# Modulation products of a two-layer hybrid backbone: units of 256 columns behind every second block instead of units of 128 behind every block

## The chip, the cores and the metric

The kernel runs on one core of one Trainium2 chip. Times are device microseconds (us) of that core; the metric is the median time of several executions. Traces are of single executions, and "span" is the time in the trace from the first to the last instruction. The engines are called PE (TensorE), DVE (VectorE), ACT (ScalarE), POOL (GpSimd) and SP (the queue from which nearly all transfers are issued).

## The reference, cut to what matters

Two layers work on 512 latent and 256 context tokens of width 1024. Each layer normalizes its input, applies a modulation, projects it, runs three mixers side by side (mLSTM, attention, gated DeltaNet), merges them, and runs a gated MLP. The modulation comes from one small vector for the latent tokens and one for the context tokens:

```python
silu_c = jax.nn.silu(c)                    # (1, 1024)
silu_cc = jax.nn.silu(c_ctx)               # (1024,)
for l in range(2):
    m_lat = split(silu_c  @ ada_w[l] + ada_b[l], 6)   # ada_w[l]: (1024, 6144)
    m_ctx = split(silu_cc @ ada_w[l] + ada_b[l], 6)
    xn = modulate(rmsnorm(h, norm1_w[l]), m[0], m[1])
    h = h + m[2] * merge_branches(...)
    h = h + m[5] * conv_ffn(modulate(rmsnorm(h, norm2_w[l]), m[3], m[4]), ...)
```

All of it is float32. The two modulation vectors of a layer are products of a 2 x 1024 with a 1024 x 6144 matrix: 24 MB of weights per layer for two rows of output. The products of the tokens (768 rows) with the other weights are the large products.

## The kernel before, in words

**Large products.** `gemm_fm` (L227) walks over blocks of 128 output columns. For each block it loads the weights into a buffer of the ring `wraw` (L207, three buffers of 128 x 1024 float32), splits them into a high and a low part (ACT and DVE), and issues three matmuls per 128 rows of depth (`mm3`, L241; the lines L248, L249 and L250): high x high, high x low and low x high, over 512 latent columns and, where the context is needed, 256 context columns. `gemm_first` and `gemm_tail` (L283 to L285, L313 to L315) do the same at the ends of a stage.

**Modulation products.** The first 16 groups of 128 columns of layer 0 are computed at the start in four pieces of 512 columns (`ada_mm`, L438, transposed at L449). The other 80 groups stand in a list, `adaq`, and each is a *unit* (`ada_unit`, L457): one load of 512 KB (1024 rows by 128 columns, runs of 512 bytes) into a buffer of the same ring `wraw`; eight matmuls (L467), which hold 32 columns of the condition vectors as the stationary operand and stream 128 columns of weights, each on one of four strips of 32 columns of the array, so that four of them run side by side; and a copy by ACT (L470) of the 128 x 128 result from PSUM to SBUF. Each matmul of float32 is two passes in the trace, so a unit is 16 rows of PE. The unit is finished by `ada_fin` (L481), which is called at the beginning of the next unit: one transpose on PE (L489), and on DVE a sum over the four strips (L491) and, after every eighth group, the bias.

**Where the units stand.** A counter, `nada`, is set ahead of a stage, and `gemm_fm` issues one unit behind each block of large products until it is zero: 32 in the mixers of layer 0, 16 in the MLP of layer 0, 20 in the mixers of layer 1. `ada_fill(4)` (L473) issues four units in a row at three places: after each layer's merge, and at the start of layer 1's mixers. That makes the 80. The results of a unit go into the PSUM buffers `pc` (one buffer, which the large products of the mixers use for the context) and, for the transposes, `pl` or `pa`.

**What sets the order.** Apart from the start, the order of instructions on each engine is written out by a planner when the program is built: it simulates the engines with a cost of its own for each instruction and takes, at each step, the instruction of the highest priority that is ready. In the mixers the recurrences and the attention have a higher priority than the large products and the units, so their small matmuls are put between the matmuls of a unit wherever the planner has them ready; a unit is then *cut* into pieces. On the chip each engine executes its list in order.

**Names in the rows.** `ad` is the loaded weight buffer of a unit, `adp` the PSUM result of its matmuls, `adr` the copy, `adc` the transposed result, `ada` the modulation vector. `mg`, `cz`, `ao`, `aq`, `ak` are large products of the mixers, `f0...` those of layer 0's MLP, `b0...` attention, `c0...` gated DeltaNet, `m0...` mLSTM (0 is the layer).

Of the kernel before, what the change touches and what calls it, by code (L numbers as in the profile page):

```python
# [19 lines left out]
DEPTH = 2  # L20
NT = SEQ + CTX
KD = D // 128
# [71 lines left out]
class Kernel:  # L94
# [112 lines left out]

    def wraw(self, src, nk, ncols, nm, slot=None):

        t = slot(nm) if slot else self.T([128, 1024], nm, tag="wraw", bufs=3)  # L210
        v = t[:, : nk * ncols].rearrange("p (k c) -> p k c", k=nk)
        with self.high(self.prio):
            self.nc.sync.dma_start(v, src.rearrange("(k p) c -> p k c", p=128))
        return v
# [12 lines left out]
    def gemm_fm(self, src, c0, ncols, nk, segs, done, nm):  # L227

        for b in range(ncols // 128):
            raw = self.wraw(src[:, c0 + 128 * b: c0 + 128 * b + 128], nk, 128, f"{nm}r{b}")
            hv, lv = self.wsplit(raw, nk, 128, f"{nm}s{b}")
            done(b, self.mm3(hv, lv, nk, segs, f"{nm}p{b}"))
            if self.nada:
                self.nada -= 1
                self.ada_unit()
                if self.nada == 0:
                    self.ada_fin()

    def mm3(self, hv, lv, nk, segs, nm):  # L241
        nc = self.nc
# [214 lines left out]
    def ada_unit(self):  # L457


        nc = self.nc  # L460
        l, g = self.adaq.pop(0)
        raw = self.wraw(self.I["ada_w"][l][:, 128 * g:128 * g + 128], KD, 128, f"ad{l}_{g}")
        self.ada_fin()
        ps = self.adps[0](f"adp{l}_{g}")
        for k in range(KD):
            j = k % 4
            nc.tensor.matmul(ps[32 * j:32 * j + 32, 0:128], self.s32[:, 2 * k:2 * k + 32], raw[:, k, :],  # L467
                             start=(k < 4), stop=(k >= 4), tile_position=(0, 32 * j))
        rw = self.T([128, 128], f"adr{l}_{g}", tag="adr")
        nc.scalar.copy(rw, ps[:, 0:128])  # L470
        self.adal = (l, g, rw)

    def ada_fill(self, n):  # L473

        if n:
# [2 lines left out]
                self.ada_unit()  # L478
            self.ada_fin()

    def ada_fin(self):  # L481

        nc = self.nc
        if self.adal is None:
            return
        l, g, rw = self.adal
        self.adal = None
        ps = self.adps[1](f"adc{l}_{g}")
        nc.tensor.transpose(ps[:, 128:256], rw, self.ident)  # L489
        a = self.ada[l][:, g:g + 1, :]  # L490
        nc.vector.tensor_reduce(out=a, in_=ps[:, 128:256].rearrange("p (o j r) -> p o r j", o=1, j=4)[:, :, 0:2, :],  # L491
                                axis=AX.X, op=ALU.add)
        if g % 8 == 7:
            a = self.ada[l][:, g - 7:g + 1, :]
            bb = self.vcol("ab", 48 * l + g - 7, 8)
            nc.vector.tensor_tensor(out=a, in0=a, in1=bb.rearrange("p (b o) -> p b o", o=1).broadcast_to([128, 8, 2]),
                                    op=ALU.add)

# [166 lines left out]
    def gates_mm(self, l, xs, gc):  # L665

        nc = self.nc
        nm = f"g{l}"
        W = self.I["w_in"][l]
        n = 288  # L670
        h, lo = [self.gw(f"{nm}w{u}", u).rearrange("p (k c) -> p k c", k=KD) for u in range(2)]
        for k0 in (0, 3, 6):
            nk = min(3, KD - k0)
            raw = self.T([128, 1024], f"{nm}raw{k0}", tag="wraw", bufs=3)[:, :nk * n].rearrange("p (k c) -> p k c", k=nk)
            rows = W[128 * k0:128 * (k0 + nk), :].rearrange("(k p) c -> p k c", p=128)
            for o, c0, m in ((0, A_G, 16), (16, C_G, 16), (32, B_Q + 512, 256)):
                nc.sync.dma_start(raw[:, :, o:o + m], rows[:, :, c0:c0 + m])
            self.split(h[:, k0:k0 + nk], lo[:, k0:k0 + nk], raw)
        self.bp = self.dr.tile([6, 128, 768], F32, name=f"bp{l}", tag=f"bp{l}")

        banks = ((self.pb, self.pb, self.pl), (self.pl, self.pc, self.pb)) if l else ((self.pl, self.pl, self.pc),) * 2
        for r in range(2):
            pss = [p(f"{nm}ps{r}_{i}")[:, 0:n] for i, p in enumerate(banks[r])]
            for i, ps in enumerate(pss):
                tt = 3 * r + i
                (a, _), xh, xl = xs[tt // 4]
                t = slice(128 * tt - a, 128 * tt - a + 128)
                for k in range(KD):
                    nc.tensor.matmul(ps, xh[:, k, t], h[:, k, :], start=(k == 0), stop=False)
                    nc.tensor.matmul(ps, xl[:, k, t], h[:, k, :], start=False, stop=False)  # L690
                    nc.tensor.matmul(ps, xh[:, k, t], lo[:, k, :], start=False, stop=(k == KD - 1))
                nc.vector.tensor_copy(gc[:, tt, :], ps[:, 0:32])
                if tt % 2 == 0:
                    s = self.gs(f"{nm}kv{tt}")
                nc.scalar.copy(s[:, 256 * (tt % 2):256 * (tt % 2) + 256], ps[:, 32:n])
                if tt % 2:
                    nc.sync.dma_start(self.bp[tt - 1:tt + 1, :, 512:768].rearrange("t p c -> p t c"),
                                      s.rearrange("p (t c) -> p t c", t=2))
# [1072 lines left out]
    def start(self):  # L1771

        nc = self.nc
        self.setup()
        self.load_x()
        self.adaq = [(l, g) for l in range(DEPTH) for g in range(48)][16:]
        xs = self.N["xs"]
        ws = []

        def weights(q):  # L1780
            raw = self.wraw(self.I["w_in"][0][512 * q:512 * q + 512, C_K:C_K + 256], 4, 256, f"c00kr{q}")
            ws.append(self.wsplit(raw, 4, 256, f"c00ks{q}", nc.gpsimd))

        self.fw = lambda k, b: [w[:, k % 4, 128 * b:128 * b + 128] for w in ws[k // 4]]
        segs = [(a, a + 256) for a in (0, 256, 512)]
        self.ada_mm(0, 2)
        self.norm_t(2)
        self.ada_red(0, 2)
        self.ada_mm(0, 0)
        weights(0)  # L1790
        self.ada_red(0, 0)
        self.mod_half(0)
        self.first_open(xs, "c00k")
        for i in (0, 1):
            self.norm_half(0, *segs[i])
            self.norm_low(0, *segs[i])
            self.first_part(xs, KD, 0, 4, *segs[i])
        self.norm_half(0, *segs[2])
        self.ada_mm(0, 3)
        self.spill_h(0, NT, nc.scalar)  # L1800
        self.norm_low(0, *segs[2])
        weights(1)
        self.ada_mm(0, 1)
        self.ada_red(0, 3)
        self.first_part(xs, KD, 0, 2, *segs[2])
        self.ada_red(0, 1)
        self.mod_half(1)
        self.first_part(xs, KD, 2, 4, *segs[2])
        for seg in segs:
            self.norm_half(1, *seg)  # L1810
            self.norm_low(1, *seg)
            self.first_part(xs, KD, 4, 8, *seg)

    def body(self):
        nc, tc = self.nc, self.tc
        with tc.tile_pool(name="t0", bufs=1, reuse_waits="tile") as self.ph:
            with tc.manual_schedule(engines={E.PE, E.DVE, E.Activation}):
                self.start()
            xs = self.N["xs"]
        for l in range(DEPTH):  # L1820
            nt = NT if l < DEPTH - 1 else SEQ
            with tc.tile_pool(name=f"m{l}", bufs=1, reuse_waits="tile") as self.ph:
                self.px = self.pc
                if l:
                    self.ada_fill(4)
                self.mixers(l, xs, nt)
            for i, k in enumerate(("ya", "yb", "yc")):
                if f"{k}{l}" in self.dbg:
                    nc.sync.dma_start(self.dbg[f"{k}{l}"][:, :, :nt], self.yd[i][:, :, :nt])
            with tc.tile_pool(name=f"t{l + 1}", bufs=1, reuse_waits="tile") as self.ph:  # L1830
                self.px = self.pb
                xs = self.merge(l, xs, nt)
                self.dump_h(f"h{l}", nt)
                if l + 1 < DEPTH:
                    self.ada_fill(4)
                    self.nada, self.adps = 16, (self.pc, self.pa)
                else:
                    self.ada_fill(4)
                self.spare = nt < NT
                xs = self.ffn(l, xs, nt)  # L1840
                self.dump_h(f"hf{l}", nt)
                if l + 1 < DEPTH:
                    self.spill_h(l + 1, NT, nc.sync)
# [80 lines left out]
```

## Time and profile before

| | |
|---|---|
| three executions | median 2715.18 us (2710.06 to 2716.42) |
| the profiled execution | 2712.51 us |
| its span | 2710.7 us |
| PE busy | 2640.8 us, 97% of the span |
| DVE, ACT, POOL busy | 58%, 37%, 10% |
| matmul rows of the units (L467) | 1280, 66.8 us busy |
| transposes of the units (L489) | 80 |
| loads of the units | 80 of 512 KB (96 with those of the start) |

Busy time of a group is the time covered by at least one of its instructions, so four matmuls side by side count once. The start times of consecutive rows of PE tell more than their durations: an instruction's row goes on after the next one has begun. "Idle before" is the time the engine stood still ahead of an instruction, and the name behind the arrow is what ended it.

### The profile page before, as it was taken

How to read it: one execution, taken by the hardware profiler on the slowest of the kernel's cores; microseconds unless marked ns; L12 is line 12 of the kernel's file. 1: busy time of each engine (PE TensorE's matmuls, PEld its weight loads, DVE VectorE, ACT ScalarE, POOL GpSimd, SP SyncE). 2: the span in 40 equal slices, each digit the busy share in tenths (PEclk: the TensorE clock that was granted, in tenths of full speed). 3: DMA queues.
4: the chain of work that ended last, by engine and by line, in shares of the span. 5: the costliest groups of instructions: out<-in, count | busy, mean ns of one | idle time of the engine just before them, and what ended most of it. 6: DMA issues, size and time to landing. Idle time of an engine off the chain costs nothing.

```text
span 2710.7 us, 46057 instructions
## 1 busy us (share of the span) xinstructions
PE 2640.8 (97%) x18041; PEld 2252.5 (83%) x18041; DVE 1576.0 (58%) x3517; ACT 1000.3 (37%) x2269; POOL 267.0 (10%) x262
## 2 busy tenths in 40 slices
PE   7999999999999999999999999999999999999999
PEld 5887988788888888888888889788877878888887
DVE  6676655756424656444444486766677646655555
ACT  4434355333322234232232254434633332433332
POOL 1000000000210410010010120000000103100000
PEclk9999999999999999999999999999999999999999
DMA  7354332556647423412212153522377675333332
GB/s 273 96 165 137 87 109 81 148 149 189 195 137 247 140 77 113 135 53 79 63 51 75 53 151 110 159 73 78 96 195 212 175 235 161 116 96 93 94 98 86
DMA packets 526187, 344.29 MB, mean 127 GB/s; under 512 B 48167, under 2 KB 491281, under 8 KB 525201
## 3 DMA queue, kind: packets, MB, share of 16 engines
q1 hardware_dynamic: 525681, 338.19, 42.6%
q8 instruction: 142, 2.33, 0.3%
q10 hardware_dynamic: 288, 3.15, 0.3%
q14 instruction: 76, 0.62, 0.1%
HBM read 285.23 MB, written 56.03 MB: 126 GB/s over the span
## 4 chain that ended last, share of the span: by engine, by line
PE 84%; DMA 7%; DVE 6%; ACT 1%; issue 1%; SPq 1%; POOL 0%; ACTq 0%; DVEq 0%; POOLq 0%
PE mg04p L248 2%; PE mg04p L250 2%; PE mg04p L249 2%; PE adp L467 2%; PE y0p L248 1%; PE y0p L249 1%; PE y0p L250 1%; PE mg14p L248 1%; PE mg14p L250 1%; PE mg14p L249 1%; PE y1p L248 1%; PE y0op L248 1%; PE y0op L250 1%; PE y0op L249 1%; PE y1p L249 1%
## 5 line engine op out<-in xcount | busy, mean ns | idle before, releaser
L1723 POOL TENSOR_TENSOR f0a<-f0a,f0g 128x768 f32<-128x768 f32 x22 | 40.6, 1848 | 486.4 <-DVE f0a L1711 486.4
L467 PE MATMUL adp<-ad,s 128*32 128x128 f32 x1280 | 66.8, 282 | 4.4 <-DVE cz0t L904 2.4
L1723 POOL TENSOR_TENSOR f1a<-f1a,f1g 128x512 f32<-128x512 f32 x22 | 28.5, 1294 | 313.3 <-DVE f1a L1711 303.5
L467 PEld LDWEIGHTS adp<-ad,s 128*32 128x32 f32 x1280 | 34.1, 109 | 28.1 <-issue 9.5
L1725 DVE TENSOR_TENSOR f0gl<-f0a,f0gh 128x768 fp32r<-128x768 f32 x22 | 21.1, 958 | 61.4 <-ACT f0gh L1724 61.3
L1724 ACT CAST f0gh<-f0a 128x768 fp32r<-128x768 f32 x22 | 18.4, 835 | 80.0 <-POOL f0a L1723 80.0
L1647 POOL TENSOR_TENSOR y0a<-y0a,y0g 128x768 f32<-128x768 f32 x16 | 33.0, 2063 | 128.0 <-DVE y0g L1644 125.7
L902 ACT ACTIVATE mg0t<-mg04p 128x512 f32<-128x512 f32 (+1 forms) x40 | 19.4, 486 | 40.6 <-PE mg04p L250 31.9
L470 ACT COPY adr<-adp 128x128 f32<-128x128 f32 x80 | 21.2, 265 | 33.4 <-PE adp L467 32.8
L1647 POOL TENSOR_TENSOR y1a<-y1a,y1g 128x512 f32<-128x512 f32 x16 | 23.9, 1494 | 75.6 <-DVE y1g L1644 75.3
L1717 ACT ACTIVATE f0g<-f0g 128x768 f32<-128x768 f32 x22 | 18.5, 846 | 32.9 <-DVE f0g L1711 32.9
L998 POOL TENSOR_TENSOR m0qz<-m0qz,m0e 64x512 f32<-64x512 f32 x12 | 15.4, 1282 | 151.9 <-DMA m0e<-g0rd 115.2
L1644 DVE SCALAR_TENSOR_TENSOR y0g<-y0g,y0p 128x512 f32<-128x512 f32 (+1 forms) x32 | 17.4, 550 | 15.4 <-PE y0p L250 14.6
L1717 ACT ACTIVATE f1g<-f1g 128x512 f32<-128x512 f32 x22 | 13.8, 632 | 32.9 <-DVE f1g L1711 32.9
L491 DVE TENSOR_REDUCE ada<-adc 128x2 f32<-128x8 f32 x80 | 12.9, 161 | 21.6 <-PE adc L489 21.3
L987 DVE SCALAR_TENSOR_TENSOR m0mb<-m0mb,g0a,cst 128x128 f32<-128x128 f32 x48 | 14.1, 346 | 18.7 <-DMA m0mb<-g0rd 18.6
L1668 DVE SCALAR_TENSOR_TENSOR hr<-y0op,y0gh,hr 128x512 f32<-128x512 f32 (+1 forms) x16 | 9.8, 615 | 21.1 <-PE y0op L250 21.1
L489 PE MATMUL adc<-cst,adr 128*128 128x128 f32 x80 | 21.9, 273 | 0.0
L1620 DVE TENSOR_TENSOR y0l<-y0ld,y0h 128x768 fp32r<-128x768 f32 x12 | 13.0, 1093 | 12.6 <-ACT y0h L1619 12.5
L1011 PE MATMUL m0n<-m0vb,m0mb 128*128 128x129 f32 x96 | 18.1, 279 | 1.2 <-issue 1.2
L1743 DVE SCALAR_TENSOR_TENSOR hr<-f0d4p,ada,hr 128x512 f32<-128x512 f32 (+1 forms) x16 | 9.9, 618 | 15.7 <-PE f0d4p L250 15.7
L1743 DVE SCALAR_TENSOR_TENSOR hr<-f0d8p,ada,hr 128x512 f32<-128x512 f32 (+1 forms) x16 | 9.9, 618 | 15.7 <-PE f0d8p L250 15.7
(3924 smaller groups left out, 9948.7 us busy)
## 6 DMA issues: line engine op xcount, KB each, us to landing
ad<-ada_w SPq DMA_DIRECT2D x96, 512.0 KB, 4.1
mg04r<-w_in SPq DMA_DIRECT2D x20, 512.0 KB, 4.2
mg14r<-w_in SPq DMA_DIRECT2D x20, 512.0 KB, 4.7
y0g<-mg SPq DMA_DIRECT2D x24, 384.0 KB, 3.7
mg<-mg0t SPq DMA_DIRECT2D x24, 256.0 KB, 2.3
y0r<-w_branch SPq DMA_DIRECT2D x12, 512.0 KB, 4.7
mg<-mg1t SPq DMA_DIRECT2D x24, 256.0 KB, 3.4
y1r<-w_branch SPq DMA_DIRECT2D x12, 512.0 KB, 4.2
```

The costliest lines, as they stand in the source:

```text
L248: nc.tensor.matmul(o, hv[:, k, :], xh[:, k, :], start=(k == 0), stop=False)
L249: nc.tensor.matmul(o, hv[:, k, :], xl[:, k, :], start=False, stop=False)
L250: nc.tensor.matmul(o, lv[:, k, :], xh[:, k, :], start=False, stop=(k == nk - 1))
L467: nc.tensor.matmul(ps[32 * j:32 * j + 32, 0:128], self.s32[:, 2 * k:2 * k + 32], raw[:, k, :], start=(k < 4), stop=(k >= 4), tile_position ...
L470: nc.scalar.copy(rw, ps[:, 0:128])
L489: nc.tensor.transpose(ps[:, 128:256], rw, self.ident)
L902: nc.scalar.activation(s, o, AF.Tanh, scale=0.5)
L1647: nc.gpsimd.tensor_tensor(out=a[:, :nt], in0=a[:, :nt], in1=gt[:, :nt], op=ALU.add)
L1717: nc.scalar.activation(a[:, :nt], a[:, :nt], AF.Silu)
L1723: nc.gpsimd.tensor_tensor(out=a[:, :nt], in0=a[:, :nt], in1=keep[b][:, :nt], op=ALU.mult)
L1725: nc.vector.tensor_tensor(out=gl[:, k, :nt], in0=a[:, :nt], in1=gh[:, k, :nt].bitcast(F32), op=ALU.subtract)
L1743: nc.vector.scalar_tensor_tensor(out=hv[:, a:b], in0=ps, scalar=self.ada[l][:, 40 + j, (a >= SEQ):(a >= SEQ) + 1], in1=hv[:, a:b], op0=ALU ...
```

## The change

A unit is made twice as wide: 256 columns of the modulation weights, loaded in two transfers of 512 rows each (512 KB each, runs of 1024 bytes). Its eight matmuls stream 256 columns instead of 128, ACT copies 128 x 256, PE makes two transposes and DVE sums both in one instruction. There are 40 such units instead of 80. A unit stands behind every second block of large products (the counter keeps its values 32, 16 and 20 and counts blocks), `ada_fill` is called with 2 instead of 4, and the ring `wraw` has four buffers instead of three.

```diff
-        t = slot(nm) if slot else self.T([128, 1024], nm, tag="wraw", bufs=3)
+        t = slot(nm) if slot else self.T([128, 1024], nm, tag="wraw", bufs=4)
...
             done(b, self.mm3(hv, lv, nk, segs, f"{nm}p{b}"))
-            if self.nada:
-                self.nada -= 1
-                self.ada_unit()
-                if self.nada == 0:
-                    self.ada_fin()
+            self.ada_next()
...
-        raw = self.wraw(self.I["ada_w"][l][:, 128 * g:128 * g + 128], KD, 128, f"ad{l}_{g}")
+        W = self.I["ada_w"][l]
+        raws = [self.wraw(W[512 * q:512 * q + 512, 256 * g:256 * g + 256], 4, 256, f"ad{l}_{g}_{q}") for q in range(2)]
         self.ada_fin()
         ps = self.adps[0](f"adp{l}_{g}")
-        for k in range(KD):
-            j = k % 4
-            nc.tensor.matmul(ps[32 * j:32 * j + 32, 0:128], self.s32[:, 2 * k:2 * k + 32], raw[:, k, :],
-                             start=(k < 4), stop=(k >= 4), tile_position=(0, 32 * j))
-        rw = self.T([128, 128], f"adr{l}_{g}", tag="adr")
-        nc.scalar.copy(rw, ps[:, 0:128])
+        for q, raw in enumerate(raws):
+            for j in range(4):
+                k = 4 * q + j
+                nc.tensor.matmul(ps[32 * j:32 * j + 32, 0:256], self.s32[:, 2 * k:2 * k + 32], raw[:, j, :],
+                                 start=(q == 0), stop=(q == 1), tile_position=(0, 32 * j))
+        rw = self.T([128, 256], f"adr{l}_{g}", tag="adr")
+        nc.scalar.copy(rw, ps[:, 0:256])
...
+    def ada_next(self):
+        if self.nada:
+            self.nada -= 1
+            if self.nada % 2:
+                self.ada_unit()
+            if self.nada == 0:
+                self.ada_fin()
...
-        nc.tensor.transpose(ps[:, 128:256], rw, self.ident)
-        a = self.ada[l][:, g:g + 1, :]
-        nc.vector.tensor_reduce(out=a, in_=ps[:, 128:256].rearrange("p (o j r) -> p o r j", o=1, j=4)[:, :, 0:2, :],
+        for b in range(2):
+            nc.tensor.transpose(ps[:, 256 + 128 * b:384 + 128 * b], rw[:, 128 * b:128 * b + 128], self.ident)
+        nc.vector.tensor_reduce(out=self.ada[l][:, 2 * g:2 * g + 2, :],
+                                in_=ps[:, 256:512].rearrange("p (o j r) -> p o r j", o=2, j=4)[:, :, 0:2, :],
                                 axis=AX.X, op=ALU.add)
-        if g % 8 == 7:
+        if g % 4 == 3:
...
-        self.adaq = [(l, g) for l in range(DEPTH) for g in range(48)][16:]
+        self.adaq = [(l, g) for l in range(DEPTH) for g in range(24)][8:]
...
-                    self.ada_fill(4)
+                    self.ada_fill(2)
```

## Rows read from the trace of the kernel before

**Rows 1.** The page: busy time, share of the span and instructions of each engine
```profile
PE 2640.8 (97%) x18041; PEld 2252.5 (83%) x18041; DVE 1576.0 (58%) x3517; ACT 1000.3 (37%) x2269; POOL 267.0 (10%) x262
```

**Rows 2.** The page: the chain that ended last, share of the span by engine
```profile
PE 84%; DMA 7%; DVE 6%; ACT 1%; issue 1%; SPq 1%; POOL 0%; ACTq 0%; DVEq 0%; POOLq 0%
```

**Rows 3.** Stages: stretch, its us, busy us per engine (instructions), clock, DMA share, GB/s
```profile
185.00:760.00 575.00, 555.65 (x4783) 472.80 (x4784) 353.30 (x976) 233.78 (x696) 36.89 (x42) 0.99 0.49 139
760.00:1010.00 250.00, 250.00 (x1490) 221.39 (x1490) 115.15 (x176) 67.40 (x111) 49.73 (x32) 1.00 0.47 151
1945.00:2165.00 220.00, 210.23 (x1746) 169.03 (x1744) 148.51 (x448) 79.89 (x224) 21.37 (x28) 0.99 0.70 194
```

**Rows 4.** The page's groups: operation, tiles, count | busy us, mean ns | idle before
```profile
L467 PE MATMUL adp<-ad,s 128*32 128x128 f32 x1280 | 66.8, 282 | 4.4 <-DVE cz0t L904 2.4
L470 ACT COPY adr<-adp 128x128 f32<-128x128 f32 x80 | 21.2, 265 | 33.4 <-PE adp L467 32.8
L491 DVE TENSOR_REDUCE ada<-adc 128x2 f32<-128x8 f32 x80 | 12.9, 161 | 21.6 <-PE adc L489 21.3
```

**Rows 5.** PE in order of time, one whole unit in the MLP: start, us, instruction
```profile
1070.53 0.28 PE L250 MATMUL f0g02p<-n01xh,f0g02s1l 128*128 128x256 f32 x1
1070.65 0.27 PE L489 MATMUL adc<-cst,adr 128*128 128x128 f32 x1
1070.85 0.65 PE L467 MATMUL adp<-ad,s 128*32 128x128 f32 x16
1071.42 0.50 PE L248 MATMUL f0a02p<-n01xh,f0a02s0h 128*128 128x512 f32 x1
1071.76 0.40 PE L249 MATMUL f0a02p<-n01xl,f0a02s0h 128*128 128x512 f32 x1
```

**Rows 6.** PE in order of time, 32 passes of 512 columns at the start
```profile
42.09 3.64 PE L438 MATMUL ad<-ad,s 128*32 128x512 f32 x32
45.66 0.66 PE L449 MATMUL adc<-cst,adr 128*128 128x128 f32 x4
46.08 0.37 PE L283 MATMUL c00kp<-n00xh,c00ks0h 128*128 128x256 f32 x1
46.28 0.28 PE L284 MATMUL c00kp<-n00xh,c00ks0l 128*128 128x256 f32 x1
```

**Rows 7.** PE in order of time, one unit of the mixers cut into three pieces
```profile
268.50 0.39 PE L250 MATMUL ak0p<-n00xh,ak0s1l 128*128 128x512 f32 x1
268.73 0.40 PE L248 MATMUL ak0p<-n00xh,ak0s1h 128*128 128x512 f32 x1
269.06 0.41 PE L467 MATMUL adp<-ad,s 128*32 128x128 f32 x4
269.40 0.71 PE L1436 MATMUL c00sp<-c00v,c00kL 128*128 128x128 f32 x4
...
270.94 0.41 PE L467 MATMUL adp<-ad,s 128*32 128x128 f32 x2
271.27 0.66 PE L1220 MATMUL b0a5pp<-cst,b0a5P 128*128 128x128 f32 x4
271.86 0.62 PE L467 MATMUL adp<-ad,s 128*32 128x128 f32 x10
272.41 0.50 PE L249 MATMUL ak0p<-n00xl,ak0s1h 128*128 128x512 f32 x1
```

**Rows 8.** PE in order of time: the first and the last of the 121 pieces
```profile
187.10 0.64 PE L467 MATMUL adp<-ad,s 128*32 128x128 f32 x16 [2.40 <-DVE cz0t L904]
2342.24 0.64 PE L467 MATMUL adp<-ad,s 128*32 128x128 f32 x16
```

**Rows 9.** Waits of PE around the units: us in total, times, longest
```profile
PE adp L467 <- DVE cz0t L904: 2.4, 1, 2.4
PE adp L467 <- ACT mg0t L902: 1.2, 1, 1.2
PE adp L467 <- DMA ad<-ada_w: 0.8, 1, 0.8
```

**Rows 10.** Waits of SP's queue: us in total, times, longest
```profile
SPq L213 <- PE adp L467: 225.4, 54, 26.5
```

**Rows 11.** The page's transfers: issues, KB each, us to landing
```profile
ad<-ada_w SPq DMA_DIRECT2D x96, 512.0 KB, 4.1
```

**Rows 12.** ACT's copy of 512 columns at the start: min/median/max ns
```profile
L441 ACT COPY adr<-ad x4: 571/586/586, 23.3 to 46.0; 128x512 f32<-128x512 f32 x4
```

More of the change, by code (lines that the diff above doesn't have):

```diff
@@ L488, in ada_fin @@
         ps = self.adps[1](f"adc{l}_{g}")
-        nc.tensor.transpose(ps[:, 128:256], rw, self.ident)
-        a = self.ada[l][:, g:g + 1, :]
-        nc.vector.tensor_reduce(out=a, in_=ps[:, 128:256].rearrange("p (o j r) -> p o r j", o=1, j=4)[:, :, 0:2, :],
+        for b in range(2):
+            nc.tensor.transpose(ps[:, 256 + 128 * b:384 + 128 * b], rw[:, 128 * b:128 * b + 128], self.ident)
+        nc.vector.tensor_reduce(out=self.ada[l][:, 2 * g:2 * g + 2, :],
+                                in_=ps[:, 256:512].rearrange("p (o j r) -> p o r j", o=2, j=4)[:, :, 0:2, :],
                                 axis=AX.X, op=ALU.add)
-        if g % 8 == 7:
-            a = self.ada[l][:, g - 7:g + 1, :]
-            bb = self.vcol("ab", 48 * l + g - 7, 8)
+        if g % 4 == 3:
+            a = self.ada[l][:, 2 * g - 6:2 * g + 2, :]
+            bb = self.vcol("ab", 48 * l + 2 * g - 6, 8)
             nc.vector.tensor_tensor(out=a, in0=a, in1=bb.rearrange("p (b o) -> p b o", o=1).broadcast_to([128, 8, 2]),
@@ L673, in gates_mm @@
             nk = min(3, KD - k0)
-            raw = self.T([128, 1024], f"{nm}raw{k0}", tag="wraw", bufs=3)[:, :nk * n].rearrange("p (k c) -> p k c", k=nk)
+            raw = self.T([128, 1024], f"{nm}raw{k0}", tag="wraw", bufs=4)[:, :nk * n].rearrange("p (k c) -> p k c", k=nk)
             rows = W[128 * k0:128 * (k0 + nk), :].rearrange("(k p) c -> p k c", p=128)
@@ L1834, in body @@
                 if l + 1 < DEPTH:
-                    self.ada_fill(4)
+                    self.ada_fill(2)
                     self.nada, self.adps = 16, (self.pc, self.pa)
                 else:
-                    self.ada_fill(4)
+                    self.ada_fill(2)
                 self.spare = nt < NT
```

## The prediction

> **What bounds the kernel now.** I read the page's engine totals first: PE is busy for 97% of the span, DVE for 58% and ACT for 37% [rows 1]. The chain of waits says the same, with 84% of it on PE [rows 2]. Then I split the span by stage. Where only large products run, PE has no free time at all: 250.00 of 250.00 us [rows 3]. In the two mixer stages, which hold 52 of the 80 units, it is busy for 555.65 of 575 and 210.23 of 220 us [rows 3]. The clock is full there (0.99 to 1.00), so what a unit costs is PE time at one clock, and time saved on PE moves everything behind it forward, except the little that falls next to the 19 and 10 us of idle time in the mixers. Last I read PE in order of time around single units, because the question is what a unit takes from the stream of large products, and busy time (66.8 us for L467 [rows 4]) doesn't answer that: it leaves out the disturbance of the neighbours.
>
> **What a unit costs, from start times.** In the MLP a unit runs undisturbed [rows 5]. The transpose starts at 1070.65, the unit's first matmul 0.20 us later, the next large product 0.57 us after that, and its successor 0.34 us on, where two such products of 512 columns normally stand 0.23 us apart (268.50 and 268.73 [rows 7]). So the unit's own 16 passes take 0.57 us and the way back into large products 0.10 to 0.11. The way in is seen where no transpose stands ahead: 268.73 to 269.06 is 0.33 us instead of 0.23, so about 0.09. The transpose alone is then 0.20 - 0.09 = 0.11 us.
>
> How does 0.57 depend on the width? Call a *round* up to four matmuls side by side with both their passes; a unit is two rounds. At 128 columns two rounds take a + 2r = 0.57. At 512 columns 32 passes, four rounds of 4r each, take 45.66 - 42.09 = 3.57 = a + 16r [rows 6]. Hence r = 0.214 us and a fixed a = 0.14 us per uninterrupted run, whatever its width. A check: the piece with one round in [rows 7] takes 269.40 - 269.06 = 0.34, and a + r = 0.35. A run of q rounds therefore takes from the stream 0.33 + 0.214 q us at 128 columns (0.33 is a plus the way in and out), and at 256 columns, interpolated between the two widths measured, 0.33 + 0.428 q. The fixed 0.33 us belongs to entering and leaving, not to a number of columns or instructions.
>
> The Trainium skill says why (TensorEngine Tiling, Tiling Modes, Key Properties): changing the tiling mode of the array drains TensorE, and the units use strips of 32 columns between products that use the whole array. By that rule, halving the units helps only as far as it halves the switches, and each place where a unit is cut by other work pays the switch again. The pieces with 2 and 4 passes agree: 0.33 and 0.34 us for an eighth and a quarter of a unit.
>
> **The sum.** The units of before are 121 uninterrupted runs, of which the first and the last are shown [rows 8]: 54 whole units and 67 pieces, because other work of the mixers cuts in 41 times (22 in layer 0's mixers, 17 in layer 1's, 2 elsewhere). Together they have 193 rounds (160 would do), since a cut in the middle of a round makes two of it. Before: 121 x 0.33 + 193 x 0.214 = 81.2 us. After, with X cuts that split a round as often as now (33 of 41, 0.8): (40 + X) x 0.33 + (80 + 0.8 X) x 0.428 = 47.4 + 0.672 X.
>
> Transposes: 80 of 0.11 us, 8.8 us. After, 40 pairs. Four in a row start at 45.66 and the next product at 46.08, with its successor 0.20 instead of 0.12 later [rows 6], so four cost 0.50; one is 0.11 between large products and each further one in a row about 0.11, the first of a row 0.17. A pair is then 0.22 to 0.28; I take 0.28, 11.2 us, a loss of 2.4.
>
> The gain is 81.2 - 47.4 - 2.4 - 0.672 X = 31.4 - 0.672 X. Without any cuts before or after it would be 40 x (2 x 0.33 - 0.33) less 2.4, about 11 us.
>
> **How many cuts.** This is the unknown. A unit has seven places between its matmuls, so 560 now and 280 afterwards; 41 of 560 are cut. But what cuts in arrives by time, and a matmul of 256 columns lasts twice as long, so the chance per place nearly doubles, from p to 2p - p². Averaged over the mixers (p about 0.11) X is 39; where several cuts fall into one unit, as in [rows 7], with p near 0.3, it is 0.85 of 41, or 35. The cuts sit mostly in such contested stretches, so I take X = 35: a gain of 7.9 us. The ends are X = 20 (the halved number of places decides) with 18 us, and X = 59 with a loss of 8.3; the break-even is 47.
>
> **Waits at the units.** PE stood still 4.4 us ahead of units [rows 4], on the eviction of the single `pc` buffer and once on a load [rows 9]. Half as many units means half as many such meetings; two of three vanish at best (3.6 us), and at worst a longer copy lets the next user of `pc` wait longer. ACT's copy is 265 ns for 128 columns [rows 4] and 586 for 512 [rows 12], so about 370 for 256, 105 ns more, 40 times: a loss of at most 4.2 us if nothing covered it. A block of latent products stands between the copy and the next use of `pc`, so I take a gain of 2.
>
> **Transfers and SP.** There are 80 loads of 512 KB as before, 4.1 us to landing [rows 11]; only the runs are longer. SP's queue waits 225.4 us in total for buffers that a unit's matmuls hold [rows 10], with the weights of large products and the stores queued behind. Now two of four buffers belong to a unit instead of one of three, and the unit comes every second block, so a block's weights no longer take the buffer of the unit just ahead. PE met a late load once, 0.8 us [rows 9]. The bounds are 0.8 gained and, if each of the ten new units of layer 1's mixers (DMA share 0.70 [rows 3]) met such a wait, 8 lost; I take 0, the row being a single one.
>
> **DVE and ACT.** DVE's 80 sums of 161 ns [rows 4] become 40 about as long, ACT's 80 copies 40: some 6 us less on each, beside PE, worth nothing. The transposes wait for the copy two blocks later instead of one; at the end of a stage one block stands between them. That cover is a block of 4 us or more against a copy of 0.4; without it the loss would be 0.4 us at three places.
>
> Forecast: 7.9 + 2 = 9.9 us less, 2712.51 to 2702.6 for the profiled execution. Its time lies 2.7 below the median of the three runs, so for the median I say 2705.
>
> **The rivals.** (1) *Fewer cuts*, X of 27 or less, because half the places are offered: 31.4 - 0.672 x 23 + 2 = 18 us, 2697. For it: two halves of a cut instruction can't be cut. Against it: the cuts come by time.
>
> (2) *The gain is given back.* X stays at 41 (gain 3.9), and part of the saving becomes idle time in the mixers, where recurrences set the pace at places (9.8 us idle in 1945 to 2165 [rows 3]): with a quarter of the units there, up to 2 us are lost. Net 2 to 4 us, 2712. For it: the planner fills by its own costs and doesn't know the switch. Against it: large products fill those stretches until their end, so a shorter filler moves the end.
>
> (3) *Slower: the units are shredded.* A wide unit occupies the planner's PE longer per matmul, and attention and DeltaNet pieces of higher priority cut in at nearly every place in the mixers. Each cut costs 0.67 us now instead of 0.33 + 0.8 x 0.214 = 0.50. It decides from X = 47; at X = 62 the loss is 10 us, 2725. For it: the price per cut rises by a third, and 26 units in the mixers offer 182 places. Against it: that needs one in three of these cut, now it is one in nine.
>
> (4) *The change doesn't do what it says*, if the planner puts other work between the two transposes or between the two halves of all 40 units (X = 40 at round ends, where a cut costs 0.33 alone): 31.4 - 0.33 x 40 - 0.672 x 20 + 2 = 7 us. That is near the forecast's low end and has no case of its own.
>
> **How the numbers follow.** About 0.3%, or 8 us, is what a measurement can tell from no change. The forecast's case (X of 28 to 38, gain 8 to 14) has 0.45, the first rival 0.12, the second 0.34, the third 0.09. Faster is 0.57, same 0.34, slower 0.09. The range leaves out the upper part of the first rival and most of the third: 2693 to 2717; the forecast's own is 2700 to 2708. The planner writes a new order for the whole of the mixers, and their 29 us of idle time can move by a few us either way; that is why the range goes 2 above the time before.
>
> **What would show it.** L467 with 640 rows and about 75 runs instead of 121; a whole unit of 1.00 us from its first matmul to the next product; pairs of transposes 0.37 us ahead of a unit; stretches without units as long as before; PE idle still near 65 us in the mixers and the start together. Wrong would be: a whole unit well above 1.0 us (the cost then goes with the columns), more than 47 cuts, or waits of PE for `ad` or `adr` that weren't there.

## The result and the profile after

The changed kernel takes 2688.68 us (median of 4 executions, 2685.60 to 2692.11) against 2714.64 for the kernel before (4 executions): a ratio of 0.9907, 95% interval 0.9889 to 0.9925, or 26 us faster. Measured once more on another chip (e1 below) it was 0.9930 [0.9918, 0.9943], 19 us. Forecast were 2705 and a gain of 10, with 2693 as the lower end of the range. The direction was right, the size was about twice what I said, and the time lies outside the range. One execution of e9 (3051 us, at a granted clock of 0.81) and one of the kernel before beside it (3357 us, at 0.72) stand apart from all others and are left out of every number below.

The page after, engine totals, the groups of the units and the loads, to be held against [rows 1, 4, 11]:

```profile
PE 2626.6 (98%) x17401; PEld 2242.8 (83%) x17401; DVE 1567.7 (58%) x3477; ACT 993.6 (37%) x2229; POOL 268.0 (10%) x262
...
L465 PE MATMUL adp<-ad,s 128*32 128x256 f32 x640 | 52.5, 399 | 0.0
...
L468 ACT COPY adr<-adp 128x256 f32<-128x256 f32 x40 | 14.9, 372 | 16.8 <-PE adp L465 15.9
...
ad<-ada_w SPq DMA_DIRECT2D x96, 512.0 KB, 3.8
```

The units' matmuls (now L465) have 640 rows, 52.5 us busy instead of 66.8, and PE no longer stands still ahead of any of them: 0.0 instead of 4.4. ACT's copy takes 372 ns; 370 was expected.

PE after, in order of time, one whole unit in the MLP, the counterpart of [rows 5]:

```profile
1044.71 0.28 PE L246 MATMUL f0g02p<-n01xh,f0g02s0l 128*128 128x256 f32 x1
1044.83 0.38 PE L497 MATMUL adc<-cst,adr 128*128 128x128 f32 x2
1045.14 1.07 PE L465 MATMUL adp<-ad,s 128*32 128x256 f32 x16
1046.14 0.50 PE L244 MATMUL f0g02p<-n01xh,f0g02s1h 128*128 128x512 f32 x1
1046.48 0.39 PE L245 MATMUL f0g02p<-n01xl,f0g02s1h 128*128 128x512 f32 x1
```

From the unit's first matmul to the next large product it is 1046.14 - 1045.14 = 1.00 us, as worked out from the two other widths, and 0.34 to its successor as before. The pair of transposes stands 0.31 us ahead, not 0.37: a second transpose costs 0.11 and not 0.17.

The stages after (stretch, its us, busy us per engine with instructions, clock, DMA share, GB/s), for [rows 3]:

```profile
185.00:760.00 575.00, 562.07 (x4620) 480.27 (x4619) 346.34 (x958) 232.47 (x682) 36.36 (x40) 0.99 0.49 143
...
1935.00:2150.00 215.00, 206.80 (x1573) 165.60 (x1572) 140.26 (x402) 75.54 (x185) 20.72 (x27) 0.98 0.70 197
```

In layer 0's mixers PE is idle for 12.9 us instead of 19.3; in layer 1's for 8.2 of 215 instead of 9.8 of 220. In the whole span it is idle for 63.8 us instead of 69.9. Of the 20.4 us between the two spans, 17 had been won when layer 0's MLP began (its first product waits until 1012.20 before and 995.49 after), and 2 more by its end.

A count in the rows of PE gives the number that the prediction turned on. Before there were 121 uninterrupted runs of unit matmuls in 80 units, 41 cuts. Now there are 55 runs in 40 units: 15 cuts, and 91 rounds. I had taken 35 cuts and allowed 20 to 59.

The clock was not the same in the two traces. TensorE is granted one of two levels, 2.4 or 1.2 GHz, and a matmul takes longer at the lower one. In e3 (below), PE in order of time at the lower level, and the stretch around it (us, busy us of PE, weight loads, DVE, ACT and POOL, clock, DMA share, GB/s):

```profile
2195.19 0.80 PE L248 MATMUL mg10p<-n10xh,mg10s2h 128*128 128x512 f32 x1 [5.79 <-ACT mg1t L903]
2196.20 0.63 PE L250 MATMUL mg10p<-n10xh,mg10s2l 128*128 128x512 f32 x1
2196.63 0.63 PE L248 MATMUL mg10p<-n10xh,mg10s2h 128*128 128x512 f32 x1
...
2195.00:2200.00 5.00, 4.81 (x11) 3.84 (x12) 2.72 (x4) 3.00 (x6) 0.00 (x0) 0.50 0.71 192
```

Two such products stand 0.43 us apart here and 0.23 at the higher level [rows 7], so of the time that PE is busy at the lower level 46% is lost. By the clock records of the traces PE was busy at that level for 24.5 us before and for 43.1 after, an estimated loss of 11.2 and 19.7 us. Below, *PE's work* is its busy time less this loss: 2629.6 us before and 2606.9 after. The 20.4 us between the spans are thus 22.7 less work and 6.1 less idle time, with 8.5 given back to the lower clock.

### The profile page after: what moved, and what is told of

The parts are those of the page before. It is cut to its first block, busy times and chain, and to the rows that moved or that the text cites. A ratio compares the mean times of both kernels' runs of the same rounds, so it can differ in the third digit from the quotient of the medians.

```text
span 2690.3 us, 44642 instructions
## 1 busy us (share of the span) xinstructions
PE 2626.6 (98%) x17401; PEld 2242.8 (83%) x17401; DVE 1567.7 (58%) x3477; ACT 993.6 (37%) x2229; POOL 268.0 (10%) x262
## 4 chain that ended last, share of the span: by engine, by line
PE 85%; DVE 6%; DMA 5%; issue 1%; ACT 1%; SPq 1%; POOL 0%; DVEq 0%; POOLq 0%; ACTq 0%
PE mg04p L246 2%; PE mg04p L245 2%; PE mg04p L244 2%; PE adp L465 1%; PE y0p L244 1%; PE y0p L246 1%; PE y0p L245 1%; PE mg14p L244 1%; PE mg14p L246 1%; PE mg14p L245 1%; PE y1p L244 1%; PE y1p L245 1%; PE y1p L246 1%; PE y0op L245 1%; PE y0op L244 1%
## 5 line engine op out<-in xcount | busy, mean ns | idle before, releaser
L465 PE MATMUL adp<-ad,s 128*32 128x256 f32 x640 | 52.5, 399 | 0.0
L465 PEld LDWEIGHTS adp<-ad,s 128*32 128x32 f32 x640 | 18.0, 111 | 18.5 <-issue 7.7
L1725 ACT ACTIVATE f0g<-f0g 128x768 f32<-128x768 f32 x22 | 18.5, 845 | 32.5 <-DVE f0g L1719 32.5
L910 ACT ACTIVATE mg0t<-mg04p 128x512 f32<-128x512 f32 (+1 forms) x40 | 19.4, 487 | 20.9 <-PE mg04p L246 19.9
L1751 DVE SCALAR_TENSOR_TENSOR hr<-f0d0p,ada,hr 128x512 f32<-128x512 f32 (+1 forms) x16 | 9.9, 617 | 21.0 <-PE f0d0p L246 21.0
L995 DVE SCALAR_TENSOR_TENSOR m0mb<-m0mb,g0a,cst 128x128 f32<-128x128 f32 x48 | 13.7, 346 | 14.3 <-DMA m0mb<-g0rd 14.2
L468 ACT COPY adr<-adp 128x256 f32<-128x256 f32 x40 | 14.9, 372 | 16.8 <-PE adp L465 15.9
L1751 DVE SCALAR_TENSOR_TENSOR hr<-f0d12p,ada,hr 128x512 f32<-128x512 f32 (+1 forms) x16 | 9.9, 617 | 15.7 <-PE f0d12p L246 15.7
L1627 ACT CAST y0h<-y0ld 128x768 fp32r<-128x768 f32 x12 | 10.0, 833 | 23.3 <-DMA y0ld<-m0y 13.2
L1019 PE MATMUL m0n<-m0vb,m0mb 128*128 128x129 f32 x96 | 17.6, 275 | 0.3 <-DVE m0mb L998 0.3
```

The costliest lines, as they stand in the source:

```text
L465: nc.tensor.matmul(ps[32 * j:32 * j + 32, 0:256], self.s32[:, 2 * k:2 * k + 32], raw[:, j, :], start=(q == 0), stop=(q == 1), tile_positio ...
L910: nc.scalar.activation(s, o, AF.Tanh, scale=0.5)
L1019: nc.tensor.matmul(o, Ps[d][:, h, :], v[:, h, :], start=True, stop=first)
L1725: nc.scalar.activation(a[:, :nt], a[:, :nt], AF.Silu)
L1751: nc.vector.scalar_tensor_tensor(out=hv[:, a:b], in0=ps, scalar=self.ada[l][:, 40 + j, (a >= SEQ):(a >= SEQ) + 1], in1=hv[:, a:b], op0=ALU ...
```

## The experiments

Each kernel was timed in five rounds against the kernel before on the same chip, in four groups (e1 to e4, e5 to e8, e9 to e12, e13 to e15). "us" is the difference of the two medians. The last three columns are of the one traced execution, in us: PE's idle time, the loss to the lower clock, and PE's work, which add up to the span. Of one program they can be told to some 2 us: the change and e1 differ by 1.8 in work, the kernel before, e5 and e10, whose units differ little, by 1.5.

| kernel | runs of units | median | ratio to before, 95% | us | idle | clock | work |
|---|---|---|---|---|---|---|---|
| before | 121 | 2714.64 | | | 69.9 | 11.2 | 2629.6 |
| the change | 55 | 2688.68 | 0.9907 [0.9889, 0.9925] | -26.0 | 63.8 | 19.7 | 2606.9 |
| e1 the change again | 55 | 2691.03 | 0.9930 [0.9918, 0.9943] | -18.6 | 64.8 | 17.4 | 2608.7 |
| e2 narrow matmuls | 75 | 2692.03 | 0.9937 [0.9925, 0.9949] | -17.6 | 61.0 | 13.1 | 2616.1 |
| e3 before, uncut | 79 | 2706.16 | 0.9983 [0.9974, 0.9991] | -3.5 | 68.9 | 18.5 | 2616.5 |
| e4 change, uncut | 41 | 2686.89 | 0.9912 [0.9897, 0.9927] | -22.8 | 66.5 | 19.0 | 2599.9 |
| e5 before, ring of 4 | 118 | 2712.48 | 1.0004 [0.9993, 1.0015] | +0.7 | 62.1 | 20.9 | 2628.1 |
| e6 change, ring of 3 | 58 | 2697.72 | 0.9954 [0.9939, 0.9969] | -14.1 | 68.9 | 13.0 | 2614.0 |
| e7 change, other parity | 60 | 2694.02 | 0.9943 [0.9925, 0.9961] | -17.8 | 65.2 | 13.7 | 2610.6 |
| e8 512 columns | 30 | 2723.89 | 1.0055 [1.0038, 1.0073] | +12.1 | 91.8 | 25.7 | 2604.3 |
| e9 two narrow in a row | 91 | 2726.49 | 1.0066 [1.0051, 1.0082] | +18.2 | 84.1 | 27.7 | 2616.7 |
| e10 before, late | 126 | 2709.05 | 0.9999 [0.9987, 1.0011] | +0.7 | 61.5 | 13.5 | 2628.9 |
| e11 change, late | 56 | 2683.36 | 0.9904 [0.9888, 0.9921] | -24.9 | 58.5 | 13.1 | 2610.1 |
| e12 e7 with ring of 3 | 59 | 2715.31 | 1.0020 [1.0006, 1.0033] | +7.0 | 79.8 | 19.8 | 2613.2 |
| e13 e11, uncut | 40 | 2680.45 | 0.9896 [0.9878, 0.9914] | -28.4 | 61.5 | 15.4 | 2602.9 |
| e14 e10, uncut | 80 | 2692.49 | 0.9947 [0.9929, 0.9965] | -16.4 | 65.3 | 12.4 | 2609.7 |
| e15 e2, uncut | 40 | 2694.43 | 0.9950 [0.9934, 0.9966] | -14.4 | 69.5 | 22.9 | 2598.9 |

**What cuts, and what a cut costs (e1 to e4).**

> The changed kernel once more, as the yardstick for the kernels run with it. All theories: 26 us below the kernel before, give or take 3.

Measured: 19 us below before, 4 less than that allows. PE's work is the change's to 2 us.

e2 issues every wide matmul as two of 128 columns:

```diff
-            for j in range(4):
-                nc.tensor.matmul(ps[32 * j:32 * j + 32, 0:256], ..., raw[:, j, :], start=(q == 0), ...)
+            for u in range(2):
+                for j in range(4):
+                    nc.tensor.matmul(ps[32 * j:32 * j + 32, 128 * u:128 * u + 128], ...,
+                                     raw[:, j, 128 * u:128 * u + 128], start=(q == 0 and u == 0), ...)
```

> The changed kernel with every matmul of 256 columns issued as two of 128; places, loads, ring, copy and transposes stay. Theory A (a price per uninterrupted run, 0.33 us, and per round of four, 0.214 us at 128 columns and 0.428 at 256): the planner's order has 75 runs and 184 rounds of 128 columns, 64.2 us, against 55 runs and 91 rounds of 256, 57.1 us: 7 us slower than the changed kernel. Theory B (the price is one per instruction, since the change halved them from 1280 to 640 passes): nearly all of the gain goes, some 20 to 24 us slower than the changed kernel. Theory C (the gain beyond the forecast came from a lucky new order of the other work): no rule, within 10 us either way.

Measured: 1 us behind e1, the intervals overlapping. Theory B falls, which wanted 20 us or more. Theory A's 7 us don't show in the time, but they do in PE's work, 7.4 us above e1's; 3.8 us less idle time and 4.3 less loss to the clock hide them. The count of cuts says more. The same 40 units in the same places, with 15 places between matmuls instead of 7, were cut 35 times instead of 15. Per place that is 35 of 600 against 15 of 280, about one in 18 both times. In these two kernels the cuts went by places and not by time.

e3 and e4 keep all other work out of a unit once its first matmul has run:

```diff
-            nc.tensor.matmul(ps[32 * j:32 * j + 32, ...
+            with self.high(200000 if k else 0):
+                nc.tensor.matmul(ps[32 * j:32 * j + 32, ...
```

> The kernel before with one thing changed: the last seven matmuls of a unit have a priority above all other work, so the planner cuts nothing in; 80 units of 128 columns, ring of three. Theory A: 79 runs instead of 121 and 160 rounds instead of 193, 60.3 us instead of 81.2: 21 us faster than before, close to the changed kernel without any wider unit. Theory B: the instructions are as many as before, no gain (within 4 us of before). Theory C: the order of the rest is rewritten too, within 10 us of before either way.

> The changed kernel with the last seven matmuls of a unit at a priority above all other work. Theory A: 41 runs instead of 55 and 80 rounds of 256 columns instead of 91, 47.8 us instead of 57.1: 9 us faster than the changed kernel, 35 faster than before. Theory B: same as the changed kernel, within 3 us. Theory C: within 10 us of it either way.

Measured: e3 gains 3.5 us and not 21, e4 4 us on e1 and not 9. The units themselves do what the price says. Their groups on PE (operation, tiles, count | busy us, mean ns | idle before) in e3, e4, e13 and e14:

```profile
L468 PE MATMUL adp<-ad,s 128*32 128x128 f32 x1280 | 53.3, 286 | 2.5 <-DVE cz0t L905 2.1 <-ACT adr L471 0.4
```
```profile
L466 PE MATMUL adp<-ad,s 128*32 128x256 f32 x640 | 44.8, 398 | 0.0
```
```profile
L467 PE MATMUL adp<-ad,s 128*32 128x256 f32 x640 | 43.2, 388 | 0.0
```
```profile
L471 PE MATMUL adp<-ad,s 128*32 128x128 f32 x1280 | 52.1, 281 | 1.2 <-ACT mg0t L906 1.2
```

Without cuts the narrow units fall from 66.8 to 53.3 us busy, the wide ones from 52.5 to 44.8. Measured from start to start, e3's units take 11.0 us less for 42 runs fewer, 0.26 a cut; the prediction's own part was 0.14 + 0.8 x 0.214 = 0.31. The whole kernel gained a third of that, because the clock took the rest: PE's work is 13.1 us less than before, 0.31 a cut, while the lower clock cost 7.3 us more. That is not one execution's chance: the mean granted clock was 0.9911 over e3's twelve executions and 0.9934 over the seventeen of the kernel before beside them. e4's work is 8.8 us below e1's, 0.63 for each of 14 runs fewer.

So each cut of a narrow unit that went gave about the 0.31 of the unit's own time; little of the way in and out (0.19 us) that I charged to it came with it. The attention and DeltaNet pieces that had cut into a unit now stand between large products. With the units' rows left out, PE goes 610 times from matmuls of the large products' lines to others or back in the kernel before, and 594 times in e3. And a way out is paid where no unit is near, as in the trace of the change:

```profile
195.55 0.28 PE L245 MATMUL cz00p<-n00xl,cz00s1h 128*128 128x256 f32 x1
195.67 0.60 PE L1177 MATMUL b0a4pq<-cst,b0a4qs 128*128 128x128 f32 x4
196.02 0.37 PE L246 MATMUL cz00p<-n00xh,cz00s1l 128*128 128x256 f32 x1
196.23 0.28 PE L244 MATMUL cz00p<-n00xh,cz00s1h 128*128 128x256 f32 x1
196.35 0.28 PE L245 MATMUL cz00p<-n00xl,cz00s1h 128*128 128x256 f32 x1
```

Behind four matmuls on 128 x 128 the first product has its successor 0.21 us later, and that one has its own 0.12 later, so a way out of 0.09 us is paid here too.

**The ring, the place and the order (e5 to e12).**

e5 and e6 exchange the rings; e5's edit, at both places where the ring is asked for:

```diff
-        ... tag="wraw", bufs=3)
+        ... tag="wraw", bufs=4)
```

> The kernel before with four buffers in the weight ring instead of three, nothing else. By then the runs show that the units' own time on PE goes as 0.14 us per uninterrupted run plus 0.214 per round (0.428 at 256 columns), and that the way in and out, 0.19 us, is not saved when a cut goes, because the work that cut in stands elsewhere. That gives 118 runs and 193 rounds here, 57.8 us against 58.2: no change from the units. Theory R (the rest of the change's gain, some 10 us, comes from the fourth buffer, through earlier loads and less idle time of PE): 8 to 10 us faster than before. Theory O (the rest is the planner's new order as such, which any edit rewrites): anything within 7 us of before.

> The changed kernel with three buffers in the weight ring. Units' own time: 58 runs and 90 rounds of 256 columns, 46.6 us against the changed kernel's 46.6: no difference. Theory R: 8 to 10 us slower than the changed kernel, with waits of PE for weights or loads. Theory O: within 7 us of the changed kernel either way, with no wait of its own for loads.

e5 is the kernel before, to 1 us. In its trace PE is idle for 7.8 us less, which is what theory R wanted, and loses 9.7 more to the lower clock (part of that is this execution's: over all executions the mean clock was 0.9922 against 0.9933). e6 loses 7 us or more on the changed kernel (0.9954 against 0.9907 and 0.9930; its interval just overlaps e1's). So the fourth buffer gives no time to units with one load, and units with two seem to lose some without it. In e6's trace PE is idle for 68.9 us instead of 63.8, but none of it ahead of a unit, and its work is 5 to 7 us more; whether the ring or the order made it, this run alone doesn't say.

e7 puts the units behind the second of each two blocks (`if self.nada % 2 == 0`).

> The changed kernel with the units behind the second of each two blocks instead of the first: as many units, as wide, only the planner's order is another. 60 runs and 91 rounds, 47.3 us: 1 us slower than the changed kernel by the units' own time. What it differs beyond that measures the order itself; theory O expects up to 7 us, in idle time and in work that isn't the units'.

Measured: 17.8 us below before, 1 us less than e1 and 8 less than the change. PE's work is 2 to 4 us above theirs.

e8 has 20 units of 512 columns:

```diff
-        raws = [self.wraw(W[512 * q:512 * q + 512, 256 * g:256 * g + 256], 4, 256, ...) for q in range(2)]
+        raws = [self.wraw(W[256 * q:256 * q + 256, 512 * g:512 * g + 512], 2, 512, ...) for q in range(4)]
...
-            if self.nada % 2:
+            if self.nada % 4 == 3:
```

> Units of 512 columns behind every fourth block: 20 units of four loads each, four transposes, ring of four. 30 runs and 44 rounds of 0.856 us: own time 41.9 us, 5 us less than the changed kernel. If the way in and out (0.19 us) is saved too for each of the 25 runs that go, another 4 to 5: 5 to 10 us faster than the changed kernel. A rival: one unit takes all four buffers of the ring, and the weights of the next block come late: PE waits for loads, and it is slower than the changed kernel by 5 us or more.

The rival came, and it hides that the unit's own part came too: PE's work is 3 to 4 us below the changed kernel's. Waits of PE in the MLP of layer 0 in e8 (us in total, times, longest):

```profile
PE adc L499 <- ACT adr L470: 2.9, 4, 0.7
PE f0a02p L244 <- ACT f0a02s1h L204: 2.8, 1, 2.8
PE f0a00p L244 <- ACT f0a00s1h L204: 2.7, 1, 2.7
PE f0g00p L279 <- ACT n01xh L631: 1.9, 1, 1.9
PE f0d0p L244 <- ACT f0d0s5h L204: 1.5, 1, 1.5
PE f0d0p L244 <- ACT f0d0s1h L204: 1.3, 1, 1.3
```

PE waits for weights (`f0a02s1h` is the high part of a block, split by ACT after its load) in a stage where the changed kernel has only the wait for the norm. A unit whose four loads fill the ring keeps the next block's weights out. These waits for weights make 8 us here; PE's idle time in all is 28 us above the change's, and the lower clock costs 6 us more.

e9 has the place and the ring of the change with narrow units, two in a row:

```diff
                 self.nada -= 1
-                self.ada_unit()
+                if self.nada % 2:
+                    self.ada_unit()
+                    self.ada_unit()
```

> Units of 128 columns as before, 80 of them, but two in a row behind every second block, with the ring of four: the place and the ring of the change without its width. 91 runs instead of 121, 11 cuts instead of 41. The runs so far put a cut at about 0.1 us (76 cuts fewer or more over three kernels moved the time by 8.6 us), so the cuts are worth 3 us. Theory W (the bulk of the gain, 11 us, is one way in and out and one fixed 0.14 us less for each pair of units): 3 us faster than before, 14 or more slower than the changed kernel. Theory S (the bulk comes from where the units stand and how their loads run ahead): 12 us or more faster than before.

> The kernel before with the units of the mixers beginning two blocks later, nothing else: as many units, as wide, ring of three; 126 runs. By the units' own price 1 us slower than before. What it differs beyond that is what a rewritten order alone does; if the order is worth up to 7 us as the two traces' idle times suggest, it lies within 7 us of before, and a lucky order would show as a gain here too.

> The changed kernel with the units of the mixers beginning two blocks later: 56 runs. By the units' own price equal to the changed kernel. Theory O (the changed kernel's order is a lucky one): 5 us or more slower than it. Otherwise within 3 us.

> The kernel with the units behind the second of each two blocks, here with three buffers in the ring; 59 runs. Theory R (two loads per unit need the fourth buffer): 5 to 8 us slower than its twin with four, as the changed kernel was with three. Theory O (that loss was the order's): anywhere within 5 us of the twin.

e9 is slower than before by 18.2 us, so narrow units gain no time from the place and the ring, and theory S's 12 us didn't come. But e9 brings waits of its own, which the change doesn't have. The longest around its units are those of the first unit of a pair for the single `pc` buffer, until DVE has emptied it of a large product (7.49 us here; the kernel before has this wait once, with 2.40 us [rows 8]), and those of the transposes, which stand right behind the pair's first unit, for the copy:

```profile
187.76 1.08 PE L469 MATMUL adp<-ad,s 128*32 128x128 f32 x16 [7.49 <-DVE cz0t L906]
...
PE adp L469 <- DVE cz0t L906: 9.5, 2, 7.5
PE adc L491 <- ACT adr L472: 5.5, 10, 1.5
```

e9 is idle for 14.2 us more than before and loses 16.5 more to the lower clock (over its executions 0.9886, against 0.9939 beside it). Its work is 12.9 us less than before. So the place did give something, 30 runs fewer; the width gives the 8 to 10 us of work by which e9 still stands above the changed kernel. At the prices so far I estimate 9 for that: 40 times the fixed 0.33 is 13, less 4 because its 11 narrow cuts cost less than the change's 15 wide ones. Its 11 cuts in 560 places, one in 51, also show that the number of places alone doesn't set the cuts.

e10 and e11 begin the mixers' units two blocks later, a counter of two ahead of the first unit. Both are rewritten orders with nothing else changed: e10 lies 0.7 us from before, e11 at 0.9904, as good as the change. The change's order was no luck.

e12 loses 21 us on its twin e7, more than theory R's 8. Between the traces it is 14.6 us of idle time, 6.1 of lower clock and 2.6 of work. Waits of PE in layer 1's mixers, first e12, then e7:

```profile
PE c11vp L1434 <- ACT c11N L1607: 5.1, 1, 5.1
PE mg14p L244 <- ACT mg14s2h L204: 4.1, 1, 4.1
PE m1S L988 <- DMA m1kTb<-ak: 3.3, 1, 3.3
```
```profile
PE m1S L988 <- DMA m1kTb<-ak: 1.4, 1, 1.4
PE m1pk L944 <- DMA m1kT<-ak: 1.3, 2, 1.1
PE c11o L1568 <- issue: 1.1, 1, 1.1
```

With three buffers PE waits 4.1 us for weights of a large product (`mg14s2h`) and longer for a tile read back from memory (`m1kTb`); with four neither wait is there at that length. Twice now, about 7 and 21 us, wide units with three buffers lost what the fourth keeps. Only the second is far outside the intervals, and only there do the waits show a way.

**Cuts once more (e13 to e15).** e13 and e14 are e11 and e10 with the priority of e3; e15 is e2 with it.

> The changed kernel with its units two blocks later and no cuts: 40 runs and 80 rounds instead of 56 and about 90. If a cut costs the 0.67 us of the prediction, 16 cuts are 10 us, and it is 10 us faster than the late kernel with cuts (36 below before). If a cut costs about 0.2 us: 3 us faster. The best version so far in either case.

> The kernel before with its units two blocks later and no cuts: 80 runs instead of 126. If a cut of a narrow unit costs the 0.50 us of the prediction: 46 cuts, 23 us faster than before. If it costs 0.1 to 0.2: 4 to 9 us faster. With e13 it also shows what two whole narrow units cost more than a wide one with cuts out of play: 0.285 us for each of 40 pairs would be 11 us, and more than that is not in the prediction's sum.

> The changed kernel with every matmul as two of 128 columns and no cuts: 40 runs of 32 passes, in the places of the change. By a price per run and per column streamed it equals the changed kernel without cuts, to 1 us. A price per instruction of the size that would explain the whole gain (640 passes, 20 us) would put it 20 us behind.

e13 gains 3 us on e11 for 16 cuts, e14 17 on e10 for 46. Over the four kernels without cuts, 118 cuts fewer gave 3.5 + 17.1 + 4.2 + 3.5 = 28.3 us, 0.24 a cut, between 0.08 (e3) and 0.37 (e14). In PE's work they gave more, and more evenly: 13.1 + 19.2 us for the narrow units' 88, 0.37 a cut, and 8.8 + 7.2 for the wide units' 30, 0.53 a cut. Idle time and the lower clock took the rest back. e15's units take as long as e4's (44.1 against 44.8 us busy) and PE's work is the same to 1 us, as a price per run and per column says; yet it is 8 us behind in time. Between the traces that is 3.0 us of idle time and 3.9 of lower clock. Differences of that size come from order and clock, and they are the limit of what the times can say. e13 is the fastest kernel: 2680.45, 28 us below before.

## Why the prediction was wrong, step by step

**What bounds the kernel: right, but for "one clock".** PE's time came out of the total: 22.7 us less work between the traces, 20.9 in e1. The prediction read the clock as full from 0.99 to 1.00 and gave it no term. In the traces the lower level cost 8.5 us more after the change than before (6.2 in e1).

**What a whole unit costs: right.** 1.00 us for 256 columns, the fixed 0.33 us per run, and a gain of two units against one. In layer 0's MLP and the fill ahead of it PE's busy time fell by 2.5 us for ten wide units, 0.25 each against 0.285 forecast (0.40 with the lower clock counted out). With the cuts out of play the wide kernels (e4, e13) lie at 0.9904 of before on average and the narrow ones (e3, e14) at 0.9965: 16.5 us for 40 units. In PE's work it is 11.7, and the forecast's whole units are 11. The drain that the Trainium skill names (TensorEngine Tiling, Tiling Modes, Key Properties) is a reading of this fixed part that no run here tests by itself. e2 and e15 agree with it, since the price stayed with the run when the instructions doubled; but a way out of 0.09 us also stands behind matmuls that use the whole array (196.02 above), so at least that part of the 0.33 needs no drain.

**The step that failed: "How many cuts".** It said "what cuts in arrives by time, and a matmul of 256 columns lasts twice as long, so the chance per place nearly doubles". The chance per place did not rise: 41 of 560 before, 15 of 280 after, 35 of 600 with the same units in halves (e2). So X was 15, below the 20 that I took as the lower end. My own first rival ("half the places are offered") was the right mechanism for the change, with a chance of 0.12 and 23 cuts. Why the chance per place holds there and falls to one in 51 in e9 stays open. That the planner puts other work at a boundary when it is ready by the planner's own clock, which I took for the chip's, is a reading that no run tests.

**The price of a cut, 0.67 or 0.50 us: somewhat too high.** In PE's work it is 0.53 and 0.37: 0.13 or 0.14 less each time, because most of the way in and out, 0.19 us, isn't saved. (35 of the 41 cuts before split a round, not 33; that is 0.4 us.) With X = 15 my formula gives 31.4 - 10.1 = 21.3 us, and PE's work fell by 20.9 to 22.7. So the sum was right in the main, but for X. The forecast had the cuts as a net loss of 3 (35 x 0.67 against 41 x 0.50); at the measured prices they are a gain of 7 (41 x 0.37 against 15 x 0.53). These 10 us are the whole error against the 20 between the traces.

The other errors cancel, and that is luck. The transposes cost 0 instead of a loss of 2.4. Idle time fell by 5 to 6 us instead of 2, with the 4.4 ahead of units gone altogether. Against these gains stand the 6 to 8.5 us of lower clock.

**Transfers and SP: valued at 0.** The fourth buffer gives no time by itself (e5), and the wide units lose about 7 and 21 us without it (e6, e12). I priced the change's parts one by one and did not ask what the wide unit does without its buffer.

What also stays open: why the lower level took more time in some of these kernels than in others, where e6's extra work comes from, and the spread of the price of a cut, 0.31 and 0.42 in narrow units, 0.63 and 0.45 in wide ones, which 2 us either way in each trace would cover in part.

## What to carry to other kernels

Small matmuls on part of the array are best priced by uninterrupted run, from start times at the run's two ends, and not by busy time or by instruction. Where a planner interleaves, count the runs of the same kind in its written order before pricing them: here the count could not be had from the widths, and neither time nor the number of boundaries gave it in every kernel. Credit the end of an interruption with the interrupted work's own time; most of the way in and out was not saved. Before pricing a cause from the time, take out PE's idle time and what ran at the lower clock: e3's cuts gave 3.5 us in time and 13.1 in PE's work. A wider transfer per unit needs its place in the ring: here the wide units were worth 18 to 26 us with four buffers and between -7 and 14 with three.

## What the hardware showed that I had not expected

The ring of four has a price far from the units. With it PE has a longer wait ahead of the gate products of both layers. The gate products of layer 0 (tile `g0ps`; stretch, us, busy us of PE, weight loads, DVE and ACT, clock, DMA share, GB/s) after the change, and in e6 with three buffers:

```profile
60.00:110.00 50.00, 22.10 (x143) 20.87 (x142) 1.14 (x6) 2.19 (x6) 0.93 0.34 96
```
```profile
60.00:110.00 50.00, 20.75 (x144) 19.37 (x144) 1.03 (x6) 2.18 (x6) 1.00 0.35 96
```

PE before those products, first after the change, then in e6 (start, us, instruction, idle before):

```profile
62.38 1.12 PE L1294 MATMUL c00kp<-cst,c00kq 128*128 128x128 f32 x4 [2.28 <-DVE c00kq L1271]
65.24 0.61 PE L699 MATMUL g0ps<-g0w,n00xh 128*128 128x288 f32 x1 [1.04 <-DVE g0w L205]
```
```profile
61.80 0.66 PE L1294 MATMUL c00kp<-cst,c00kq 128*128 128x128 f32 x4 [0.73 <-DVE c00kq L1271]
62.80 0.37 PE L697 MATMUL g0ps<-g0w,n00xh 128*128 128x288 f32 x1 [0.34 <-DVE c00k0a L1267]
64.27 0.40 PE L699 MATMUL g0ps<-g0w,n00xh 128*128 128x288 f32 x1 [0.97 <-DVE g0w L205]
```

After an idle 2.28 us PE goes on at the lower of its two levels for a while (1.2 GHz; the granted clock is 0.66 in 60 to 70 us), and the four transposes take 1.12 us instead of 0.66; after an idle 0.73 it stays at 2.4 GHz. By their clock records all eleven traces with four buffers are at the lower level for 3 to 7 us from 62 to 66 us on, and none of the six with three. Not every such wait is followed by it: in the kernel before PE goes on at 2.4 GHz after an idle 2.01 us at 1592.6. From start to start the gate products of both layers cost 44.2 us instead of 40.4, and the two kernels of before with three and four buffers (40.0 and 44.8) show the same. The change pays some 4 us there, beside the idle time itself; that is about half of what it loses to the lower clock beyond the kernel before.
